# Splitting a weight once: a decoder block whose later token passes load the two parts of each weight from DRAM

## The chip, the cores and the metric

The kernel runs on one core of a Trainium2 chip. The metric is device time in microseconds (us) of one execution. Engines are named as the profile names them: PE (matmuls; PEld its weight loads), DVE (vector), ACT (scalar), POOL (GpSimd), SP (the queue that issues the DMAs).

## The reference

One conditioned decoder layer on 1024 tokens of width 1024, in float32. Cut to its matmuls and what stands between them:

```python
h = modulate(rmsnorm(x, norm1_g), sh1, sc1)
z = einsum('bsd,de->bse', h, w_in)         # pool channels | q | k | v | forget logits | gates A, B
y = sigmoid(gA) * causal_pool_mixer(u, w_pool, pool_scale) + sigmoid(gB) * forgetting_attention(q, k, v, log_f)
x = x + gt1 * einsum('bsd,de->bse', y, w_out)
h2 = modulate(rmsnorm(x, norm2_g), sh2, sc2)
q = einsum('bsd,dk->bsk', h2, w_query)     # 8 heads x 2 halves x 128
# scores against 128 sub-keys per half, top 16 of each half, top 16 of their sums: 16 of 16384 experts per head
x = x + gt2 * sum_k gelu(h2 . expert_u[idx_k]) * gate_k * expert_v[idx_k]
out = rmsnorm(x, final_g)
```

The modulation rows sh1 to gt2 are `c @ w_mod + b_mod`.

## The kernel before, in words

Float32 accuracy is had on PE by splitting each operand into a high part (ACT rounds it, line 232) and a low part (the remainder, line 233, on DVE or POOL), and by three matmuls for each product: high by high, high by low, low by high (`mm3`, lines 256 to 258).

Tokens go through the layer in three passes, `PHASES = ((0, 512), (512, 256), (768, 256))`. Each pass uses every weight of the layer once: 45 chunks of w_in, 8 of w_out, 16 of w_query. A chunk is a tile of 128 x 8 x 128 floats, 512 KB. `load_w` loads it into `wr` (line 244, two buffers), splits it into `wh` on ACT and `wl` on POOL (two buffers each; five for the head of the first pass, where the splits into `wl` run on DVE), and `proj` or `to_T` multiplies it with the tokens of the pass. So every chunk is loaded and split three times in a run, once for each pass.

A pass has a head (normalised and modulated columns, forget logits), an attention part for 8 pairs of heads (q, k, v, two gate chunks and half a pooling chunk for each pair), the output projection (into which the head of the next pass is written), and the query projection with the top-k on DVE. In the second and third pass background work is mixed in by a credit count in program order (`tick`): the choice of experts (`choose`, DVE) and the gate blocks (`gates`: products on POOL, line 942, comparisons on DVE, line 944, small matmuls and copies).

After the passes comes the dense stage: for the tokens of tiles 1 to 5 all 16384 experts are computed as dense matmuls. It uses `load_w` for 256 more chunks (`ut`, `vt`), while the experts of the other three tiles are gathered row by row in the background.

The order of instructions on each engine is set by the framework's scheduler, which orders by a timeline of its own; DMAs from SP are issued in one order, and each waits there for what it needs (buffer free, data written, and the completion of the eighth DMA before it on SP).

The names that matter below: `wr`, `wh`, `wl` (loaded chunk and its two parts), `wm` (rows of w_mod, for the modulation), line 565 (`mx`, the maximum over two parts of a score row, ahead of the exponential in line 567), line 570 (`dn`, the sum of two denominators), line 829 (`cand`, one step of the choice of experts).

Of the kernel before, what the change touches and what calls it, by code (L numbers as in the profile page):

```python
# [7 lines left out]
F = mybir.dt.float32  # L8
R = mybir.dt.float32r
# [37 lines left out]
def block_kernel(ctx: ExitStack, tc: tile.TileContext, I, out, dbg=None):  # L47
# [4 lines left out]
    dram = ctx.enter_context(tc.tile_pool(name="dram", bufs=1, space=bass.MemoryType.DRAM))  # L52
# [2 lines left out]
    psx = tc.alloc_tile_pool(name="psx", bufs=1, space=PS, reuse_waits="tile")  # L55
    sel = ctx.enter_context(tc.tile_pool(name="sel", bufs=1))
    gp = ctx.enter_context(tc.tile_pool(name="gp", bufs=1))
    W = {"i": 0, "m": 0}

    bg = {"todo": [], "credit": 0.0, "rate": 1.0}  # L60

# [98 lines left out]
    sh1, sc1, gt1, sh2, sc2, gt2 = (modc[:, 8 * i:8 * i + 8] for i in range(6))  # L160
# [66 lines left out]
    def mv(dst, src):  # L227
        fix = lambda a: a.bitcast(F) if a.dtype == R else a
        return nc.sync.dma_start(fix(dst), fix(src))

    def split(hi, lo, src, eng_lo):
        nc.scalar.activation(hi, src, AF.Copy)  # L232
        eng_lo.tensor_tensor(lo, src, hi.bitcast(F), op=OP.subtract)  # L233
# [3 lines left out]
    def wl_eng():  # L237
        wcount[0] += 1
        on_dve, per = wcount[1]
        return nc.vector if wcount[0] % per < on_dve else nc.gpsimd  # L240

    def load_w(src, eng=None):
        wr = W["p"].tile([128, 8, 128], F, name="wr", tag="wr", bufs=2)
        nc.sync.dma_start(wr, src)
        W["i"] = (W["i"] + 1) % (W["n"] + W["m"])
        wp, n = (W["p"], W["n"]) if W["i"] < W["n"] else (W["x"], W["m"])
        wh = wp.tile([128, 8, 128], R, name="wh", tag="wh", bufs=n)
        wl = wp.tile([128, 8, 128], R, name="wl", tag="wl", bufs=n)
        split(wh, wl, wr, eng or wl_eng())
        return wh, wl  # L250

    def w_row(name):
        return W["p"].tile([128, 8, 128], F, name=name, tag="wr", bufs=2).rearrange("p a b -> p (a b)")

# [11 lines left out]
    def head(p):  # L266
# [19 lines left out]
        c.tile, c.p_tile = tile_, p_tile  # L286
        c.xs = W["xs"] if p else x_rows(c)
        return c
# [42 lines left out]
    def x_cols(p, c):  # L331
        t0, n = PHASES[p]
        tiles, xs = load_cols(p, lambda: W["xq"].tile([128, D], F, name="xq", tag="xq", bufs=2))
        pt = spread(c, rs8[:, t0 // 128:(t0 + n) // 128])
# [5 lines left out]

    def to_T(c, xs, rsb, sc, sh, th, tl, srcs):

        ws = [load_w(src) for src in srcs]
        zs = [(z_tile() if i < 2 else s_tile("z"))[:, :c.n] for i in range(len(srcs))]

        def mm(k):
            for z, (wh, wl) in zip(zs, ws):
                mm3(z, wh[:, k], wl[:, k], th[:, k], tl[:, k], k == 0, k == 7)

        for k in range(8):  # L350
            full = c.tile("full", 3)
            if len(xs) < 8:
                src = pt_tile()[:, :c.n]
                for i in range(c.NQ):
                    nc.tensor.transpose(src[:, i * 128:(i + 1) * 128], xs[i][:, k * 128:(k + 1) * 128], ident)
            elif rsb is None:
                src = xs[k]
            else:
                src = full
                nc.vector.tensor_tensor(full, xs[k], rsb, op=OP.mult)  # L360
            nc.scalar.activation(full, src, AF.Identity, scale=sc[:, k:k + 1], bias=sh[:, k:k + 1])
            split(th[:, k], tl[:, k], full, nc.vector)
            if k > 1:
                mm(k - 2)
        mm(6)
        mm(7)
        return zs

    def head2(c):
        n, t0 = c.n, c.t0  # L370
        c.hTh = c.big.tile([128, 8, n], R, name="hTh", tag="A")
        c.hTl = c.big.tile([128, 8, n], R, name="hTl", tag="B")
        cols = (C_F,) + ((C_U, C_GA, C_GB, C_Q) if c.p == 0 else ())
        zs = to_T(c, c.xs, None, sc1, sh1, c.hTh, c.hTl, [I["w_in"][i] for i in cols])
        z = zs[0]
        c.pre = dict(zip(cols[1:], zs[1:]))

        zf, e1 = (c.tile("full", 3)[:16] for _ in range(2))
        nc.scalar.activation(zf, z[:16], AF.Identity, bias=bfc)
        nc.scalar.activation(e1, zf, AF.Abs)  # L380
        nc.scalar.activation(e1, e1, AF.Exp, scale=-1.0)
        nc.scalar.activation(e1, e1, AF.Ln, bias=1.0)
        nc.vector.scalar_tensor_tensor(e1, zf, 0.0, e1, op0=OP.min, op1=OP.subtract)
        nc.vector.tensor_tensor_scan(zf, e1, e1, flast, op0=OP.add, op1=OP.bypass)
        nc.vector.tensor_copy(flast, zf[:, n - 1:n])
        nc.vector.tensor_scalar(e1, zf, -1.0, None, op0=OP.mult)
        fhl = c.big.tile([48, n], R, name="fhl", tag="fhl", bufs=1)
        fh, fl = fhl[0:16], fhl[32:48]
        split(fh, fl, e1, nc.vector)
        mv(Fd[:, 0, t0:t0 + n], fh)  # L390
        mv(Fd[:, 1, t0:t0 + n], fl)
        if dbg and "F" in dbg:
            nc.sync.dma_start(dbg["F"][:, t0:t0 + n], zf)

    def proj(c, src, xh, xl):
        wh, wl = load_w(src)
        z = z_tile()[:, :c.n]
        for k in range(8):
            mm3(z, wh[:, k], wl[:, k], xh[:, k], xl[:, k], k == 0, k == 7)
        tick(24 * c.n * 0.00043)  # L400
        return z

    def w_in(c, i):
        return c.pre.pop(i) if i in c.pre else proj(c, I["w_in"][i], c.hTh, c.hTl)

    def u_unit(c, j):
        g, n = j // 2, c.n
# [50 lines left out]
    def phase(c, nxt):  # L458
        p, t0, n, NQ, qb0, KL, big = c.p, c.t0, c.n, c.NQ, c.qb0, c.KL, c.big
# [231 lines left out]
        tiles, x1 = load_cols(p, lambda: p_tile("x1"))  # L691
        ss = o_tile()[:, :n]
        sa = c.tile("sc", 1)
        for e in range(8):
            if nc_ and e == WO:
                head2(nc_)
            z = proj(c, I["w_out"][e], c.yh, c.yl)
            nc.vector.scalar_tensor_tensor(x1[e], z, gt1[:, e:e + 1], x1[e], op0=OP.mult, op1=OP.add)
            if e == 0:
                nc.scalar.activation(sa, x1[e], AF.Square)  # L700
                continue
            sq = c.tile("full", 3)
            nc.scalar.activation(sq, x1[e], AF.Square)
            if e < 7:
                nc.vector.tensor_tensor(sa, sa, sq, op=OP.add)
            else:
                nc.tensor.matmul(ss, onef, sa, start=True, stop=False)
                nc.tensor.matmul(ss, onef, sq, start=False, stop=True)
# [5 lines left out]
        rsb = rstd_T(c, ss)  # L714
        h2h = big.tile([128, 8, n], R, name="h2h", tag="A")
        h2l = big.tile([128, 8, n], R, name="h2l", tag="B")
        z0, = to_T(c, x1, rsb, sc2, sh2, h2h, h2l, [I["w_query"][0]])
        dl = [i for i in range(NQ) if DT0 <= qb0 + i < DT1]
        gl = [i for i in range(NQ) if i not in dl]
        if dl:  # L720
# [29 lines left out]
        tx = [sel.tile([128, PH, 2, 16], U32, name="mxi", tag="mxi", bufs=4) for _ in range(NQ)]  # L750
        for ch in range(16):
            h, half = ch // 2, ch % 2
            z = proj(c, I["w_query"][ch], h2h, h2l) if ch else z0
            if p == 2 and ch % 2:
                for x in range(2):
                    tc.keep_in_program_order(mv(W["h2"][x][:, ch // 2], h2dT[x][:, ch // 2]))
            q2 = c.tile("full", 3)
            nc.scalar.activation(q2, z, AF.Copy)
            ky = big.tile([128, 128], F, name="ky", tag="ky", bufs=2)
            nc.sync.dma_start(ky, I["keys"][ch])  # L760
            ps = pt_tile()[:, :n]
            for i in range(NQ):
                nc.tensor.matmul(ps[:, i * 128:(i + 1) * 128], q2[:, i * 128:(i + 1) * 128], ky,
                                 start=True, stop=True)
            sc = big.tile([128, n], F, name="sc", tag="sc", bufs=1)
            nc.scalar.activation(sc, ps, AF.Copy)
            for i in range(NQ):
                s_ = sc[:, i * 128:(i + 1) * 128]
                m_, x_ = tv[i][:, h, half], tx[i][:, h, half]
                tmp = sel.tile([128, 128], F, name="tmp", tag="tmp", bufs=2)  # L770
                nc.vector.max(m_[:, 0:8], s_)
                nc.vector.max_index(x_[:, 0:8], m_[:, 0:8], s_)
                nc.vector.match_replace(tmp, m_[:, 0:8], s_, -3e38)
                nc.vector.max(m_[:, 8:16], tmp)
                nc.vector.max_index(x_[:, 8:16], m_[:, 8:16], tmp)
        big.release()
        return nc_, [choose(qb0 + i, tv[i], tx[i]) for i in range(NQ)]

# [276 lines left out]
    c = head(0)  # L1055
# [5 lines left out]
    W["m"] = 3  # L1061
    head2(c)
    W["m"] = 0
    W["x"].release()
    u_unit(c, 0)
    g_unit(c, 0)
# [10 lines left out]
    c, ch = phase(c, next_head(1))  # L1077
# [5 lines left out]
    c, ch = phase(c, next_head(2))  # L1083
# [3 lines left out]
    c, ch = phase(c, lambda: None)  # L1087
# [66 lines left out]
```

## Time and profile before

| | before |
|---|---|
| median of 3 runs | 3461.2 us (3460.72 to 3464.09) |
| profiled execution | 3456.16 us, span 3454.5 us |
| mean granted PE clock | 0.967 |
| busy, share of the span | PE 92%, weight loads 88%, DVE 75%, ACT 39%, POOL 60% |
| HBM read, written | 778.90 MB, 77.23 MB |
| splits of weights on POOL (all stages) | 458, mean 2431 ns |
| splits of weights on ACT (all stages) | 463, mean 1059 ns |

The shares are means over the whole span. The three passes take the first 1590 us or so, the dense stage the rest; PE is busy all the time in the dense stage and less in the passes. The clock column of a view is the share of the full PE clock that was granted.

### The profile page before, as it was taken

The page shows a single profiled execution, that of the slowest core. Times are in us where ns is not written, and L with a number is a line of the kernel's source. Part 1 is how long each engine was busy: PE and PEld are TensorE (multiplying, and loading weights), DVE is VectorE, ACT ScalarE, POOL GpSimd, SP SyncE. Part 2 cuts the span into 40 slices and gives each one's busy share as a digit, 9 for nine tenths or more (in the row PEclk, how much of TensorE's full clock was granted, in tenths as well). Part 3 has the DMA queues.
Part 4 walks back from the last instruction along what each step waited for, and adds up shares of the span by engine and source line. Part 5 has one row for each costly group of instructions (what it writes and reads, how often), then busy time and mean ns, then how long its engine had stood idle before and what let it go on. Part 6 is the DMA issues. An engine that isn't in the chain of part 4 may idle for free. (4 is left out here: it accounts for less than half of the span.)

```text
span 3454.5 us, 57302 instructions
## 1 busy us (share of the span) xinstructions
PE 3179.9 (92%) x21232; PEld 3036.0 (88%) x21232; DVE 2582.4 (75%) x5472; ACT 1361.5 (39%) x2455; POOL 2089.0 (60%) x1466
## 2 busy tenths in 40 slices
PE   6999988778788789889999999999999999999995
PEld 4788777778778778879999999999999999999995
DVE  7855467998868997787876776776677767777677
ACT  5555543456565556663222222332232223222221
POOL 1233243346568445574677777777777777877774
PEclk9999999899899999989999999999999999999997
DMA  8633453345555545565698998899998998999897
GB/s 293 230 112 109 169 171 100 129 127 173 172 181 176 154 130 166 183 217 178 246 334 321 326 333 325 324 329 344 335 333 318 332 339 327 343 327 336 318 342 253
DMA packets 339095, 859.91 MB, mean 249 GB/s; under 512 B 30352, under 2 KB 146688, under 8 KB 336640
## 3 DMA queue, kind: packets, MB, share of 16 engines
q1 hardware_dynamic: 228224, 453.54, 39.5%
q0 software_dynamic: 110592, 402.70, 31.9%
q8 instruction: 168, 2.75, 0.3%
q14 instruction: 111, 0.91, 0.1%
HBM read 778.90 MB, written 77.23 MB: 248 GB/s over the span
## 5 line engine op out<-in xcount | busy, mean ns | idle before, releaser
L233 POOL TENSOR_TENSOR wl<-wr,wh 128x1024 fp32r<-128x1024 f32 x458 | 1113.1, 2431 | 851.7 <-ACT wh L232 751.4
L232 ACT ACTIVATE wh<-wr 128x1024 fp32r<-128x1024 f32 x463 | 490.0, 1059 | 1018.3 <-PE oT L257 528.8
L256 PE MATMUL oT<-ah,wh 128*128 128x320 f32 x2048 | 633.5, 310 | 5.7 <-ACT ah L232 5.7
L256 PE MATMUL z<-h2x,wh 128*128 128x320 f32 x2048 | 634.0, 310 | 1.3 <-DVE al L233 1.3
L257 PE MATMUL oT<-al,wh 128*128 128x320 f32 x2048 | 634.1, 310 | 0.2 <-DVE al L233 0.2
L258 PE MATMUL z<-h2x,wl 128*128 128x320 f32 x2048 | 634.1, 310 | 0.0
L257 PE MATMUL z<-h2x,wh 128*128 128x320 f32 x2048 | 633.9, 310 | 0.0
L258 PE MATMUL oT<-ah,wl 128*128 128x320 f32 x2048 | 633.9, 310 | 0.0
L896 DVE SCALAR_TENSOR_TENSOR acc<-g,dots,acc 128x1024 f32<-128x1024 f32 x381 | 489.6, 1285 | 113.4 <-DMA g<-peer_v,idx 110.7
L886 DVE SCALAR_TENSOR_TENSOR g<-g,h 128x1024 f32<-128x1024 f32 x384 | 461.3, 1215 | 89.4 <-DMA g<-peer_u,idx 88.3
L871 POOL DMA_INDIRECT g<-peer_u,idx x384 | 362.1, 943 | 130.0 <-issue 56.1
L871 POOL DMA_INDIRECT g<-peer_v,idx x384 | 362.0, 943 | 126.8 <-issue 46.4
L256 PE MATMUL z<-hTh,wh 128*128 128x256 f32 (+1 forms) x1080 | 365.3, 342 | 39.3 <-DVE ks L505 9.8
L256 PEld LDWEIGHTS oT<-ah,wh 128*128 128x128 f32 x2048 | 385.3, 188 | 6.2 <-ACT ah L232 6.2
L257 PEld LDWEIGHTS oT<-al,wh 128*128 128x128 f32 x2048 | 385.4, 188 | 0.9 <-DVE al L233 0.9
L256 PEld LDWEIGHTS z<-h2x,wh 128*128 128x128 f32 x2048 | 384.7, 188 | 1.5 <-DVE al L233 1.5
L258 PEld LDWEIGHTS oT<-ah,wl 128*128 128x128 f32 x2048 | 385.4, 188 | 0.0
L258 PEld LDWEIGHTS z<-h2x,wl 128*128 128x128 f32 x2048 | 384.7, 188 | 0.2 <-POOL wl L233 0.2
L257 PEld LDWEIGHTS z<-h2x,wh 128*128 128x128 f32 x2048 | 384.7, 188 | 0.0
L257 PE MATMUL z<-hTl,wh 128*128 128x256 f32 (+1 forms) x1080 | 360.7, 334 | 1.9 <-DVE hTl L233 1.9
L258 PE MATMUL z<-hTh,wl 128*128 128x256 f32 (+1 forms) x1080 | 360.8, 334 | 1.7 <-POOL wl L233 1.7
L942 POOL TENSOR_TENSOR o<-hi,lo 128x512 f32<-128x512 f32 x160 | 204.4, 1282 | 128.2 <-PE G L954 95.5
(268 smaller groups left out, 6035.0 us busy)
## 6 DMA issues: line engine op xcount, KB each, us to landing
wr<-w_in SPq DMA_DIRECT2D x135, 512.0 KB
wr<-ut SPq DMA_DIRECT2D x128, 512.0 KB
wr<-vt SPq DMA_DIRECT2D x128, 512.0 KB
Gd<-Gb SPq DMA_DIRECT2D x40, 1024.0 KB
Gg<-Gd SPq DMA_DIRECT2D x16, 2560.0 KB
wm<-w_mod SPq DMA_DIRECT2D x48, 512.0 KB
wr<-w_query SPq DMA_DIRECT2D x48, 512.0 KB
wr<-w_out SPq DMA_DIRECT2D x24, 512.0 KB
```

The source lines that it names most:

```text
L232: nc.scalar.activation(hi, src, AF.Copy)
L233: eng_lo.tensor_tensor(lo, src, hi.bitcast(F), op=OP.subtract)
L256: nc.tensor.matmul(ps, ah, bh, start=start, stop=False)
L257: nc.tensor.matmul(ps, ah, bl, start=False, stop=False)
L258: nc.tensor.matmul(ps, al, bh, start=False, stop=stop)
L871: d = nc.gpsimd.indirect_dma_start(out=g, out_offset=None, in_=table, in_offset=bass.IndirectOffsetOnAxis(ap=col, axis=0))
L886: nc.vector.scalar_tensor_tensor(g, g, 1.0, h2, op0=OP.mult, op1=OP.mult, accum_out=dots[:, k:k + 1])
L896: nc.vector.scalar_tensor_tensor(acc, g, dots[:, k:k + 1], acc, op0=OP.mult, op1=OP.add)
L942: nc.gpsimd.tensor_tensor(o2, hi[:, X, :, None].to_broadcast([128, 4, 8, 16]), lo[:, X, None, :].to_broadcast([128, 4, 8, 16]), op=OP.mult)
```

## The change

In the first pass a chunk is loaded and split as before, and both parts are then stored to DRAM tiles of their own. The store of a chunk is written in the program after the load and split of the next one (`store_parts(1)`); the last ones are flushed after the head and at the end of the pass. In the second and third pass the two parts are loaded straight into the matmul operands, two DMAs of 512 KB for each chunk, and nothing is split. The buffers used for these are those of `wh` and `wl` (two pairs) and, as a third pair, the two buffers of `wr`. The dense stage still uses `load_w` and its buffers.

```diff
+    kept, owed = {}, []
+
+    def store_parts(n=0):
+        while len(owed) > n:
+            for d, t in owed.pop(0):
+                mv(d, t)
+
+    def load_s(c, name, i):
+
+        if c.p == 0:
+            wh, wl = load_w(I[name][i])
+            kept[name, i] = [dram.tile([128, 8, 128], F, name=f"{name}{x}_{i}") for x in "hl"]
+            owed.append(list(zip(kept[name, i], (wh, wl))))
+            store_parts(1)
+            return wh, wl
+
+        W["s"] = (W["s"] + 1) % 3
+        tags = ("wr", "wr") if W["s"] == 2 else ("wh", "wl")
+        w = [W["p"].tile([128, 8, 128], R, name=tag, tag=tag, bufs=2) for tag in tags]
+        for t, d in zip(w, kept[name, i]):
+            mv(t, d)
+        return w
...
-        ws = [load_w(src) for src in srcs]
+        ws = [load_s(c, *src) for src in srcs]
...
-        wh, wl = load_w(src)
+        wh, wl = load_s(c, *src)
...
-            z = proj(c, I["w_out"][e], c.yh, c.yl)
+            z = proj(c, ("w_out", e), c.yh, c.yl)
...
+        store_parts()
         big.release()
...
     head2(c)
     W["m"] = 0
+    store_parts()
     W["x"].release()
```

Three places in the order of the instructions. First SP in the head of the first pass (`w_mod` are the rows for the modulation, `w_in` the weights). Before:

```order
L167 DMA wm_225<-w_mod 128x1024
L244 DMA wr_290<-w_in 128x1024
L244 DMA wr_296<-w_in 128x1024
L167 DMA wm_230<-w_mod 128x1024
L167 DMA wm_233<-w_mod 128x1024
L167 DMA wm_238<-w_mod 128x1024
```

and now (`w_inh_28` and `w_inl_28` are the kept parts of chunk 28):

```order
L167 DMA wm_225<-w_mod 128x1024
L229 DMA w_inh_28_284<-wh_280 128x1024
L229 DMA w_inl_28_285<-wl_281 128x1024
L244 DMA wr_296<-w_in 128x1024
L229 DMA w_inh_0_292<-wh_288 128x1024
L229 DMA w_inl_0_293<-wl_289 128x1024
L244 DMA wr_306<-w_in 128x1024
L167 DMA wm_230<-w_mod 128x1024
```

Four stores stand ahead of the next rows of w_mod, on the queue that issues both.

Second POOL in the attention part of the second pass, where the gate blocks begin (`hi`, `o2` are theirs, `wpl` is the pooling weight). Before:

```order
L233 TENSOR_TENSOR wl_7722<-wr_7719,wh_7721 128x1024
L942 TENSOR_TENSOR o2_6946<-hi_6940,lo_6941 128x512
...
L942 TENSOR_TENSOR o2_7011<-hi_6940,lo_6941 128x512
L233 TENSOR_TENSOR wpl_7795<-wpr_7792,wph_7794 128x256
L233 TENSOR_TENSOR wl_7842<-wr_7839,wh_7841 128x1024
L931 TENSOR_TENSOR hi_7227<-hi_7227,pairT_6928 128x128
L942 TENSOR_TENSOR o2_7079<-hi_7073,lo_7074 128x512
L233 TENSOR_TENSOR wl_7895<-wr_7892,wh_7894 128x1024
```

and now:

```order
L233 TENSOR_TENSOR wpl_6905<-wpr_6902,wph_6904 128x256
L955 TENSOR_TENSOR hi_7178<-hi_7178,pairT_7166 128x128
...
L966 TENSOR_TENSOR o2_7184<-hi_7178,lo_7179 128x512
...
L966 TENSOR_TENSOR o2_7237<-hi_7178,lo_7179 128x512
L233 TENSOR_TENSOR wpl_8017<-wpr_8014,wph_8016 128x256
L966 TENSOR_TENSOR o2_7247<-hi_7178,lo_7179 128x512
```

Rows that repeat the product are left out. The splits of 128 x 1024 are gone; the products of the gate blocks and the small split of the pooling weight stay.

Third SP at the end of the third pass, with what each DMA waits for (`DMAHW` is an earlier DMA; `Pool` and `PE` are the engines that must be done with the buffer; `h2x` are the columns for the dense stage, `ky` the sub-keys, `ut` the first dense weights). Before:

```order
L244 DMA wr_17171<-w_query 128x1024 [waits DMAHW0_49,Pool_49]
L760 DMA ky_17098<-keys 128x128 [waits DMAHW7_49,DMAHW6_49,PE_49]
L244 DMA wr_17223<-w_query 128x1024 [waits DMAHW1_49,Pool_49]
...
L229 DMA h2x0_15657<-h2dT0_150 128x640
...
L244 DMA wr_17289<-ut 128x1024 [waits DMAHW5_49,Pool_49]
```

and now:

```order
L229 DMA wr_17175<-w_queryh_14_5650 128x1024 [waits DMAHW6_49,PE_49]
...
L229 DMA wr_17176<-w_queryl_14_5651 128x1024 [waits DMAHW0_49]
L229 DMA wh_17225<-w_queryh_15_5720 128x1024 [waits DMAHW1_49,PE_49]
L229 DMA wl_17226<-w_queryl_15_5721 128x1024 [waits DMAHW2_49,PE_49]
L229 DMA h2x0_15705<-h2dT0_150 128x640 [waits DMAHW3_49]
...
L244 DMA wr_17289<-ut 128x1024 [waits PE_49]
```

Two loads stand where one stood, and they wait for PE instead of POOL; so does the first load of the dense stage, into a `wr` buffer that now holds a part of w_query's chunk 14.

More of the change, by code (lines that the diff above doesn't have):

```diff
@@ L57, in block_kernel @@
     gp = ctx.enter_context(tc.tile_pool(name="gp", bufs=1))
-    W = {"i": 0, "m": 0}
+    W = {"i": 0, "m": 0, "s": 0}
     bg = {"todo": [], "credit": 0.0, "rate": 1.0}
@@ L373, in head2 @@
         cols = (C_F,) + ((C_U, C_GA, C_GB, C_Q) if c.p == 0 else ())
-        zs = to_T(c, c.xs, None, sc1, sh1, c.hTh, c.hTl, [I["w_in"][i] for i in cols])
+        zs = to_T(c, c.xs, None, sc1, sh1, c.hTh, c.hTl, [("w_in", i) for i in cols])
         z = zs[0]
@@ L403, in w_in @@
     def w_in(c, i):
-        return c.pre.pop(i) if i in c.pre else proj(c, I["w_in"][i], c.hTh, c.hTl)
+        return c.pre.pop(i) if i in c.pre else proj(c, ("w_in", i), c.hTh, c.hTl)
     def u_unit(c, j):
@@ L716, in phase @@
         h2l = big.tile([128, 8, n], R, name="h2l", tag="B")
-        z0, = to_T(c, x1, rsb, sc2, sh2, h2h, h2l, [I["w_query"][0]])
+        z0, = to_T(c, x1, rsb, sc2, sh2, h2h, h2l, [("w_query", 0)])
         dl = [i for i in range(NQ) if DT0 <= qb0 + i < DT1]
@@ L752, in phase @@
             h, half = ch // 2, ch % 2
-            z = proj(c, I["w_query"][ch], h2h, h2l) if ch else z0
+            z = proj(c, ("w_query", ch), h2h, h2l) if ch else z0
             if p == 2 and ch % 2:
```

## The prediction

> **What bounds the kernel now.** I read the stretches of the run first, since the page's shares average stages with different limits. The columns are the stretch, its length, then busy time with counts of PE, weight loads, DVE, ACT and POOL, the granted clock, the DMA share and GB/s. I cut where the weights of w_out and w_query are first loaded: first pass 0 to 570 us, second 570 to 1085, third 1085 to 1590, dense stage after that.
>
> ```profile
> core 0: us, PE busy (x) PEld busy (x) DVE busy (x) ACT busy (x) POOL busy (x), PEclk, DMA share, GB/s
> 0.00:375.00 375.00, 338.94 (x1729) 276.76 (x1730) 234.77 (x450) 197.05 (x399) 104.90 (x57) 0.99 0.53 179
> 375.00:460.00 85.00, 77.25 (x392) 63.00 (x391) 42.66 (x56) 38.03 (x72) 26.78 (x12) 0.98 0.54 190
> 460.00:570.00 110.00, 101.01 (x505) 83.84 (x504) 79.45 (x409) 49.90 (x73) 42.09 (x19) 0.95 0.42 137
> 570.00:905.00 335.00, 264.23 (x1880) 249.89 (x1879) 307.77 (x942) 171.99 (x365) 159.52 (x100) 0.90 0.45 138
> 905.00:1005.00 100.00, 83.93 (x619) 79.12 (x617) 73.46 (x112) 61.36 (x100) 67.20 (x44) 0.93 0.59 178
> 1005.00:1085.00 80.00, 69.12 (x544) 66.23 (x545) 64.25 (x241) 46.31 (x78) 56.82 (x34) 0.98 0.61 190
> 1085.00:1423.00 338.00, 286.15 (x2135) 268.34 (x2135) 286.75 (x668) 200.11 (x388) 181.59 (x122) 0.92 0.53 159
> 1423.00:1494.00 71.00, 64.03 (x503) 60.08 (x502) 58.18 (x79) 43.14 (x72) 43.65 (x30) 0.98 0.57 175
> 1494.00:1590.00 96.00, 80.10 (x593) 76.17 (x594) 67.75 (x250) 54.33 (x93) 63.20 (x32) 0.91 0.73 238
> 1590.00:3454.00 1864.00, 1815.13 (x12346) 1812.58 (x12344) 1367.35 (x2269) 499.32 (x821) 1343.23 (x1024) 0.99 0.88 318
> ```
>
> The dense stage is bound by PE (97%) and the change leaves its instructions alone; it will start earlier or later as a block. The first pass is bound by PE too, at 90 to 92%. The two attention stretches of the later passes are different: from 570 to 905 DVE is busy 92% and PE 79%; from 1085 to 1423 both stand at 85%. So there the vector engine and the chains through it set the time.
>
> Next the instructions themselves, in order of time, at a place in the second pass (start, us, engine, line):
>
> ```profile
> 868.04 2.38 POOL L233 TENSOR_TENSOR wl<-wr,wh 128x1024 fp32r<-128x1024 f32 x1 [3.62 <-ACT wh L232]
> 868.10 2.34 DVE L570 TENSOR_TENSOR dn<-dn 128x1 f32<-128x1 f32 x1
> ```
>
> An addition of one element per partition takes 2.34 us, and ends 0.02 us after the split of a weight on POOL that had started 0.06 us before it. The two engines do not run these together: one holds the other off. How often that happens is in the minimum, median and maximum of a line, beside its mean in the groups (both from 570 to 1590 us; in the groups count, busy us, mean ns):
>
> ```profile
> L565 DVE TENSOR_TENSOR mx<-mx x64: 107/159/2383, 602.4 to 1445.8; 128x1 f32<-128x1 f32 x64
> L570 DVE TENSOR_TENSOR dn<-dn x64: 127/160/2343, 604.1 to 1448.6; 128x1 f32<-128x1 f32 x64
> L829 DVE SCALAR_TENSOR_TENSOR cand<-pk x192: 368/406/2636, 611.8 to 1270.7; 128x128 f32<-128x128 f32 x192
> L944 DVE TENSOR_TENSOR o<-iota,pairT x160: 664/692/2905, 725.7 to 1534.7; 128x512 f32<-128x512 f32 x160
> ...
> L944 DVE TENSOR_TENSOR o<-iota,pairT 128x512 f32<-128x512 f32 x160 | 167.8, 1052 | 34.1 <-PE G L954 33.9
> L829 DVE SCALAR_TENSOR_TENSOR cand<-pk 128x128 f32<-128x128 f32 x192 | 90.4, 608 | 0.1
> L565 DVE TENSOR_TENSOR mx<-mx 128x1 f32<-128x1 f32 x64 | 39.5, 617 | 0.5
> L570 DVE TENSOR_TENSOR dn<-dn 128x1 f32<-128x1 f32 x64 | 23.5, 368 | 21.6 <-ACT P L567 21.6
> ```
>
> Busy time less count times median is 57.1 + 12.5 + 29.3 + 13.3 = 112 us for these four lines alone, held off by weight splits or by the gating products (line 942). Done for every vector instruction of 570 to 1590 us (excess over its form's tenth percentile, put to the POOL instruction that overlaps it most), it gives 155 us held off by weight splits: 55 in 570:905, 13 in 905:1005, 13 in 1005:1085, 53 in 1085:1423, 14 in 1423:1494, 7 in 1494:1590; some 65 us more fall to other POOL work, which stays. Line 565 feeds the exponential, and PE waits for that. PE's longest waits there (total us, times, longest), and what the weights cost ACT and POOL:
>
> ```profile
> PE s L558 <- ACT P L567: 23.7, 14, 7.5
> PE s L558 <- DVE qs L493: 21.1, 5, 8.8
> PE G L954 <- ACT Gb L955: 18.5, 22, 3.7
> PE o L257 <- DVE tl L233: 18.3, 11, 4.8
> ...
> PE z L258 <- POOL wl L233: 6.9, 11, 1.2
> ...
> PE z L256 <- ACT wh L232: 5.8, 9, 1.6
> ...
> 570.00:1590.00 1020.00, 0.00 (x0) 142.70 (x135) 331.74 (x136) 0.92 0.54 165
> ```
>
> PE hardly waits for the split weights (6.9 + 5.8 us); it waits for vector results. The last row (busy DVE, ACT, POOL on the loaded weight) is the work that goes.
>
> **The change, part by part.** *Splits removed:* second and third pass use 69 weights each (45 of w_in, 8 of w_out, 16 of w_query), so 138 pairs of ACT and POOL splits go, 143 us of ACT and 332 us of POOL. Neither engine is a bound there (ACT 172 of 335, POOL 160 of 335), so the gain is what DVE and PE get: between 13 us (the direct waits) and 155 us (all held-off time on the path). How far a stretch shrinks I take from PE: in the first pass, where DVE has room, PE reaches 0.91 of a stretch (0.904, 0.909, 0.918). At 0.91, with the PE work as it is, 570:905 becomes 264.2/0.91 = 290 (45 less; DVE's own 308 − 55 = 253 fits at 87%), 905:1005 becomes 92 (8 less), 1005:1085 76 (4), 1085:1423 314 (24), 1423:1494 70 (1). The last stretch could lose 8, which I put at nothing because of its loads, below. Sum 82. Each gain is under the held-off time of its stretch.
>
> *Clock:* PE work itself shrinks where the granted clock was 0.90 and 0.92. If all of it came back, that is 10% of 264 and 8% of 286, 49 us; gaps from the remaining vector waits stay, so I take a fifth, 10 us (ends 0 and 49). The Trainium skill (TensorE: Matmul & The Clock Gate, "What's actually happening") says the clock halves after about 3.4 us of idling and returns after 3.4 us of work. By that rule alone, with most waits in the rows above averaging 1 to 4 us, shorter gaps would return most of the 49 and the sum would be some 30 us better; the trace gives the low clock only as means of stretches, so I stay with a fifth.
>
> *Stores added:* 138 stores of 524 KB, 72 MB, in the first pass. The rate that the queues reach:
>
> ```profile
> q1 hardware_dynamic: 228224, 453.54, 39.5%
> ...
> 10.00:20.00 10.00, 2.17 (x7) 1.00 (x8) 7.38 (x21) 6.21 (x16) 0.00 (x0) 1.00 0.98 366
> 20.00:60.00 40.00, 36.12 (x147) 26.55 (x147) 29.30 (x56) 21.32 (x33) 1.51 (x2) 1.00 0.87 298
> 60.00:150.00 90.00, 77.05 (x362) 60.64 (x363) 83.61 (x147) 45.63 (x90) 30.52 (x18) 0.94 0.75 262
> 150.00:375.00 225.00, 223.60 (x1217) 188.58 (x1216) 112.81 (x193) 120.22 (x254) 71.85 (x32) 1.00 0.35 113
> L244 SPq DMA_DIRECT2D wr<-w_in x17: 327/328/536, 8.9 to 148.3; - x17
> ```
>
> 453.54 MB in 39.5% of 3454.5 us is 332 GB/s for a queue kept full; 366 GB/s at a share of 0.98 is 373. The whole pass moves 179 × 375 + 190 × 85 + 137 × 110 = 98 MB now, 171 MB then: 457 to 514 us of transfers in 570, so it holds on average. Up to 150 us it does not: about 42 MB move there now, and the stores of 15 of the 17 weights loaded by then add 16 MB; 58 MB are 154 to 173 us, 4 to 23 too many. In the order the stores stand between the w_mod loads that the first normalised columns wait for, so I put the overflow on the path: 13. Behind 150 us (share 0.35, PE 99%) a weight's two stores take 1.05 MB / 332 GB/s = 3.2 us, beside its own matmuls. In 460:570 a weight has 101/16 = 6.3 us of PE; before its two buffers are overwritten the stores must have landed: I take 4 us for 375:570 (ends 0 and 25, 1 us for each of 24 weights).
>
> *Loads doubled:* 138 × 0.52 = 72 MB more in the later passes, and a load now waits for PE to be done with the weight three back, on the in-order SP queue, where a load waited for POOL before. Behind it stand keys and values of the next heads and gate blocks. 165 GB/s in 570:1590 become about 236, against 332: room on average. In 1494:1590, 238 × 96 = 22.8 MB and 14 × 0.52 = 7.3 MB are 30 MB, 91 us at 332 GB/s: that stretch cannot shrink by its 8 us. Elsewhere I take 9 us of late loads (ends 0 and 69, half a microsecond for each weight). The first weight of the dense stage now waits for PE to finish with w_query's chunk 14: 4 us once (ends 0 and 7).
>
> *Sum:* −82 − 10 + 13 + 4 + 9 + 4 = −62 us. The profiled execution took 3456.2 us (span 3454.5), 5.0 below the median 3461.2 of the three runs, so the median becomes 3399 us. From the bounds: −155 − 49 = −204 at best, −13 + 23 + 25 + 69 + 7 = +111 at worst; both ends need every term at its end.
>
> **The rivals.** *Held-off time is not on the path:* the vector instructions that are held off are mostly background (line 829) and what remains of POOL's products, which now run more densely, takes over. Then only the 13 us of direct waits and none of the clock return, against 30 us of costs: 17 us slower, 3478. Against it: DVE at 92% has nowhere to put 55 us.
> *Stores hold the buffers* (slower): in the first pass the split of a weight waits until the stores of the weight two back have landed. With PE at 90 to 99% there every microsecond of delay shows. With the 92 us of gain and the other 26 us of costs it decides from 66/64 = 1.0 us per weight for the 64 weights behind the head; at 2 us it costs 128 and the run takes 3461 − 92 + 26 + 128 = 3523. For it speaks SP, in order, waiting there for splits; against it 3.2 us of transfer under 6.3 us of PE. The Trainium skill (DMA: Bandwidth & Descriptors, "Anatomy of one DMA — SWDGE (gpsimd) path") puts about 2 us of fixed time on a transfer, most of it the confirmation of the write, heaviest in HBM. That would make 5.2 us of a pair of stores, still below 6.3, and the term would stay near its 4 us; no row here times a store.
> *Loads arrive late:* half a microsecond for each of 138 weights, 69 instead of 9, leaves a gain of 2 us: 3459, no change.
> *Larger gain:* all clock and half of the held-off time beyond my 82 come back: −62 − 39 − 37 = −138, 3323.
>
> **How the numbers follow.** Forecast (gain of 30 to 100 us) 0.62; larger gain 0.08; a gain of 7 to 30 us, part of the loads late, 0.12; no change 0.05; slower 0.13, of which held-off time 0.06 and stores 0.07. A measurement tells about 0.2%, 7 us, from no change: faster 0.82, same 0.05, slower 0.13. The range 3335 to 3450 leaves out the slower cases, no change and the far end of the larger gain.
>
> **What would show it.** In the profile after: no weight split on POOL in the second and third pass; means of lines 565 and 570 (shifted by 23 lines) near 0.2 to 0.3 us; DVE busy time of the two passes down by 130 us or more, and both passes together 70 to 95 us shorter. The first pass 10 to 25 us longer, most of it before 150 us, with a DMA share near 0.95 there. The dense stage's length within 5 us. I am wrong if lines 565 and 570 keep long maxima as often as now, if PE waits for DMA of wh, wl or wr by more than 20 us in the later passes, or if the first pass grows by over 60 us.

## The result, and the profile after

The changed kernel takes 3370.6 us (median of 4 runs, 3369.7 to 3374.2) against 3461.0 before: ratio 0.974 (95% interval 0.9726 to 0.9753), 90 us less. The forecast was 3399 us, 62 less. The profiled execution has a span of 3368.4 us, 86.1 less than before.

I cut both profiles where PE begins a stage: first pass up to its last matmul of the query projection, second and third pass up to theirs, dense stage to the end. Before (length, then busy PE, weight loads, DVE, ACT, POOL, clock, DMA share, GB/s):

```profile
0.00:580.80 580.80, 528.01 (x2674) 432.60 (x2675) 366.44 (x979) 287.26 (x547) 177.96 (x88) 0.98 0.50 171
580.80:1092.00 511.20, 413.48 (x3048) 393.24 (x3047) 442.38 (x1264) 282.48 (x542) 286.26 (x179) 0.92 0.51 156
1092.00:1591.30 499.30, 424.59 (x3182) 398.88 (x3181) 407.51 (x971) 292.47 (x545) 282.85 (x177) 0.93 0.58 176
1591.30:3454.50 1863.20, 1813.83 (x12335) 1811.28 (x12333) 1366.05 (x2260) 499.32 (x821) 1341.93 (x1024) 0.99 0.88 318
```

and after:

```profile
0.00:600.00 600.00, 538.64 (x2681) 441.89 (x2682) 355.53 (x979) 283.37 (x541) 170.32 (x89) 0.97 0.82 291
600.00:1055.90 455.90, 396.44 (x3045) 378.58 (x3044) 368.63 (x1265) 223.46 (x475) 117.70 (x104) 0.95 0.78 254
1055.90:1499.30 443.40, 402.53 (x3165) 382.56 (x3164) 329.07 (x944) 233.91 (x477) 125.67 (x111) 0.97 0.83 272
1499.30:3368.40 1869.10, 1816.21 (x12347) 1811.62 (x12345) 1370.36 (x2285) 500.03 (x824) 1343.17 (x1024) 0.99 0.88 318
```

First pass 19.2 us longer, second 55.3 and third 55.9 shorter, dense stage 5.9 longer: −86.1. In the two later passes together (1010.5 us before, 899.3 after) DVE is busy 152 us less, POOL 326 and ACT 118; PE, with all but 20 of the same 6230 matmuls, 39 less, at a clock of 0.95 and 0.97 instead of 0.92 and 0.93. DMA runs at about 0.8 in all three passes.

The lines that showed the vector engine held off, in the groups after (count, busy us, mean ns) and with minimum, median and maximum; 588 and 593 are what 565 and 570 were, 968 what 944 was:

```profile
L968 DVE TENSOR_TENSOR o<-iota,pairT 128x512 f32<-128x512 f32 x160 | 137.8, 866 | 31.3 <-PE G L978 31.0
L588 DVE TENSOR_TENSOR mx<-mx 128x1 f32<-128x1 f32 x64 | 15.4, 241 | 0.6
L593 DVE TENSOR_TENSOR dn<-dn 128x1 f32<-128x1 f32 x64 | 14.9, 233 | 25.5 <-ACT P L590 25.4
...
L588 DVE TENSOR_TENSOR mx<-mx x64: 115/155/1043, 618.8 to 1362.1; 128x1 f32<-128x1 f32 x64
L593 DVE TENSOR_TENSOR dn<-dn x64: 130/159/1021, 620.5 to 1363.8; 128x1 f32<-128x1 f32 x64
```

In these two one-element lines the maxima of 2.3 us are gone; what is left, 1.0 us, is about the length of one of POOL's gate products. Counted as in the prediction, no vector time is held off by weight splits in the later passes any more (about 155 us before), and some 66 us by the gate products (some 61 before). ACT's wait for `mx` ahead of the exponential and PE's longest waits, after (total us, times, longest):

```profile
ACT P L590 <- DVE mx L588: 38.1, 31, 3.4
```

```profile
PE G L978 <- ACT Gb L979: 13.6, 13, 3.7
PE s L581 <- ACT P L590: 10.4, 12, 3.3
...
PE s L581 <- DVE qs L516: 6.9, 1, 6.9
PE o L280 <- DVE tl L233: 6.3, 8, 1.8
PE z L279 <- DMA wh<-w_inh: 4.5, 2, 3.1
...
PE z L281 <- DMA wl<-w_inl: 3.8, 4, 2.0
PE z L279 <- DMA wh<-w_queryh: 3.5, 3, 2.0
PE z L281 <- DMA wl<-w_queryl: 2.9, 4, 0.8
...
PE z L281 <- DMA wr<-w_queryl: 1.5, 2, 1.1
```

The waits for the exponential and for vector results are a third to a half of what they were (exponential 23.7, `qs` 21.1, `tl` 18.3 us). Waits for late loads have appeared, 16 us in the rows shown.

### The profile page after: what moved, and what is told of

The parts are those of the page before. It is cut to its first block, busy times and chain, and to the rows that moved or that the text cites. A ratio compares the mean times of both kernels' runs of the same rounds, so it can differ in the third digit from the quotient of the medians.

```text
span 3368.4 us, 57444 instructions
## 1 busy us (share of the span) xinstructions
PE 3153.8 (94%) x21232; PEld 3014.7 (89%) x21232; DVE 2423.6 (72%) x5472; ACT 1240.8 (37%) x2317; POOL 1756.9 (52%) x1328
## 5 line engine op out<-in xcount | busy, mean ns | idle before, releaser
L233 POOL TENSOR_TENSOR wl<-wr,wh 128x1024 fp32r<-128x1024 f32 x320 | 776.5, 2427 | 624.8 <-ACT wh L232 553.1
L232 ACT ACTIVATE wh<-wr 128x1024 fp32r<-128x1024 f32 x325 | 344.2, 1059 | 900.4 <-PE oT L280 520.7
L279 PE MATMUL z<-hTh,wh 128*128 128x256 f32 (+1 forms) x840 | 288.9, 348 | 24.5 <-ACT hTh L232 8.3
L281 PE MATMUL z<-hTh,wl 128*128 128x256 f32 (+1 forms) x840 | 287.1, 342 | 3.8 <-DMA wl<-w_inl 3.8
L280 PE MATMUL z<-hTl,wh 128*128 128x256 f32 (+1 forms) x840 | 286.7, 341 | 1.4 <-DVE hTl L233 1.3
```

Of the source, the lines that this page charges most:

```text
L279: nc.tensor.matmul(ps, ah, bh, start=start, stop=False)
L280: nc.tensor.matmul(ps, ah, bl, start=False, stop=False)
L281: nc.tensor.matmul(ps, al, bh, start=False, stop=stop)
```

## The experiments

My theory: the later passes gain because DVE is no longer held off by POOL's splits. The rivals: relief of ACT, a shorter way of the weights to PE, or another order; and for the first pass, transfers against buffers held. "Passes" below are second plus third, cut as above: 1010.5 us before, 899.3 in the changed kernel.

How far the order alone moves a pass is seen in two kernels whose later passes have the very instructions of the kernel before (stores alone, and the w_mod background spread in the kernel before; both below): 1021.5 and 1024.8 us. Differences of up to about 14 us in the passes are therefore ascribed to nothing here. The first pass of the ten kernels that keep all stores takes 589.4 to 600.0 us (580.8 before). The kernel before, timed again beside each group of runs, took 3459.5 to 3461.7 us.

**Stores alone.** First pass as in the change, later passes load and split.

```diff
+        return load_w(I[name][i])
         W["s"] = (W["s"] + 1) % 3
```

> First pass as in the changed kernel (both parts stored, 72 MB), later passes as before (load and split again). Theory (the stores cost by transfers that do not fit into the first 150 us, and nothing later): the first pass is 19 us longer than before, as in the changed kernel (600 against 581 us), the later passes as before, 3480 us (3472 to 3488). Rival (part of the 19 us comes from the second pass's double loads inside the first pass's tail, or stores still under way disturb the second pass): 3465 to 3472, or above 3490.

Measured 3478.6 us, ratio 1.0062 (1.0040 to 1.0085), 17 us more than before. The total is as expected; the place is only partly so: the first pass takes 590.5 us (9.7 more), the later passes 1021.5 (11 more, within what the order does).

**Loads alone.** Five chunks are stored, and the later passes load these five over and over, so they work with other weights.

```diff
-            owed.append(list(zip(kept[name, i], (wh, wl))))
+            if name == "w_in" and i in (C_K + 3, C_V + 3, C_Q + 4, C_K + 4, C_V + 4):
+                kept[len(kept)] = ...
...
-        for t, d in zip(w, kept[name, i]):
+        for t, d in zip(w, kept[W["r"]]):
```

> Only five chunks are stored, in the middle of the first pass, and all 138 uses of the later passes load those five in turn, so the later passes work with other weights; same instructions, same bytes loaded. Theory (gain of the later passes and cost of the stores simply add): 3371 less 19, 3352 us (3344 to 3360), first pass within 4 us of before, second and third pass 111 us shorter than before together as in the changed kernel. Rival (the later passes gain because the first pass leaves them a better start, or the stores did not cost what the first pass lost): 3362 to 3375.

Measured 3356.5 us, ratio 0.9702 (0.9686 to 0.9719), 105 less than before. First pass 584.1, later passes 899.1, the changed kernel's to 0.2 us. So gain and cost add: −105 + 17 = −88 against −90. Without the other stores the kernel is 14 us faster.

**POOL's work put back.** In the changed kernel, for each loaded chunk:

```diff
             mv(t, d)
+        scr = gp.tile([128, D], F, name="scr", tag="g", bufs=GBUFS).rearrange("p (a b) -> p a b", b=128)
+        nc.gpsimd.tensor_tensor(scr, w[0].bitcast(F), w[1].bitcast(F), op=OP.subtract)
```

> The changed kernel, with one POOL subtraction of 128x1024 put back for each loaded chunk of the later passes; it reads the two loaded parts and writes a tile that nobody reads, so nothing waits for its result. Theory (vector instructions are held off while POOL runs such an instruction, and that set the time): 130 to 155 us of DVE time are held off again, lines for mx and dn have means of 0.4 us or more, and 80 to 115 us of the gain go: 3451 to 3486 us. Rival (the gain came from ACT being relieved, from the weights no longer passing through ACT and POOL before PE, or from the later passes' other order): 3371 to 3386 us.

Measured 3484.5 us, ratio 1.0073 (1.0049 to 1.0097): 114 us over the changed kernel, all of the gain and more. Passes 1021.1 us. Its groups, its minimum, median and maximum, and ACT's wait for `mx`:

```profile
L970 DVE TENSOR_TENSOR o<-iota,pairT 128x512 f32<-128x512 f32 x160 | 166.0, 1042 | 16.1 <-PE G L980 15.6
L590 DVE TENSOR_TENSOR mx<-mx 128x1 f32<-128x1 f32 x64 | 34.5, 539 | 0.6
L595 DVE TENSOR_TENSOR dn<-dn 128x1 f32<-128x1 f32 x64 | 26.8, 419 | 25.7 <-ACT P L592 25.4
...
L590 DVE TENSOR_TENSOR mx<-mx x64: 128/160/2310, 616.8 to 1467.9; 128x1 f32<-128x1 f32 x64
```

```profile
ACT P L592 <- DVE mx L590: 94.3, 40, 8.6
```

The maxima of 2.3 us are back, some 154 us of vector time are held off by this instruction, and ACT waits 94 us for `mx` (100.1 before, 38.1 in the changed kernel). Nothing reads what the instruction writes. POOL's own gate products queue behind it too, but PE waits only 3.6 us for them here (7.3 in the changed kernel). The theory holds; that the instruction also waits for the loads is taken up below.

**Half of it, and a copy instead.** The same with `scr[:, :4]` (128x512), and with `nc.gpsimd.tensor_copy(scr, w[0].bitcast(F))`.

> As the kernel that puts POOL's subtraction back, but on half of each chunk (128x512). Theory (time held off goes with the length of POOL's instruction): between 40 and 70 us of the 114 return, 3411 to 3441. Rival (it is the number of encounters, not their length): 90 us or more, 3461 or more.

> As the kernel that puts POOL's work back, but with a copy of one loaded part (one input) in place of the subtraction of two. If a POOL instruction holds vector instructions off for its own length whatever it is, its length in the profile gives the loss: with 1.0 to 1.3 us each, as for the half subtraction, 3411 to 3441. If only a POOL instruction with two inputs does, 3371 to 3385.

Measured 3407.6 us (ratio 0.9849, 0.9831 to 0.9868) and 3405.4 (0.9846, 0.9825 to 0.9867), 37 and 35 over the changed kernel; both fall a few us short of the expected 3411, since their first passes are 8 and 10 us shorter than the changed kernel's. The lengths of POOL's instruction:

```profile
L274 POOL TENSOR_TENSOR scr<-wh,wl 128x512 f32<-128x512 f32 x89 | 121.1, 1361 | 224.6 <-DMA wl<-w_inl 171.8 <-DMA wl<-w_queryl 41.3 <-DMA wl<-w_outl 8.6
```

```profile
L274 POOL COPY scr<-wh 128x1024 f32<-128x1024 f32 x88 | 100.8, 1146 | 241.6 <-DMA wh<-w_inh 175.2 <-DMA wh<-w_queryh 49.3 <-DMA wh<-w_outh 14.4
```

| POOL per chunk | mean length | vector time held off by it | passes | over the changed kernel |
|---|---|---|---|---|
| none | | 0 | 899.3 us | |
| copy, one input | 1.12 us | 31 us | 938.1 | 39 |
| subtraction of a half | 1.36 us | 55 us | 946.6 | 47 |
| subtraction of the whole | 2.48 us | 154 us | 1021.1 | 122 |

The loss grows with the time held off, at 0.8 to 0.9 us for each us in the two subtractions and 1.3 in the copy, where what the order may do is a third of the loss. A copy with one input holds DVE off as well.

**ACT's work put back.** `nc.scalar.activation(scr, w[0].bitcast(F), AF.Copy)` for each chunk.

> The changed kernel, with one ACT copy of 128x1024 put back for each loaded chunk of the later passes, into a tile that nobody reads (138 times 1.06 us, 146 us of ACT). Theory (ACT's time was not what the later passes gained from): at most 12 us longer, 3371 to 3383 us. Rival (ACT's relief made the exponentials and the high parts of the probabilities earlier, and this is half of the gain or more): 3415 us or more.

Measured 3404.8 us, ratio 0.9848 (0.9827 to 0.9870), 34 over the changed kernel; passes 939.0 (40 more). That is between my two cases: ACT was worth more than I gave it. Read the other way, this is the change without its gain on ACT: with POOL's splits gone and ACT's work kept (though PE no longer waits for its result), the passes are 71.5 us shorter than before, and taking ACT's work away as well gives another 39.7.

**The waits without the work.** One element per partition on POOL and on ACT for each chunk, and the same on ACT alone:

```diff
+        nc.gpsimd.tensor_tensor(scr[:, 0, :1], w[0][:, 0, :1].bitcast(F), w[1][:, 0, :1].bitcast(F), op=OP.subtract)
+        nc.scalar.activation(scr[:, 1, :1], w[0][:, 0, :1].bitcast(F), AF.Copy)
```

> The changed kernel with, for each loaded chunk of the later passes, a POOL subtraction and an ACT copy of one element per partition of the loaded tiles: the waits and the hold on the buffers of the two kernels that put the work back, without its length. Theory (the length of the work did it): within 8 us of the changed kernel, 3363 to 3379. Rival (the instructions that were put back delayed the loads, because a buffer stays taken until POOL or ACT, in order, gets to it): a third or more of the 114 us of the POOL work, 3409 or more.

> The changed kernel with only the ACT copy of one element per partition of each loaded chunk. The kernel with this and POOL's one element took 24 us more than the changed one without adding any length. Theory (ACT issues in order, so an instruction that waits there for a load keeps the exponentials and copies behind it): most of the 24 us are ACT's, 3386 to 3398 us. Rival (POOL issues in order too, and its gate products wait behind the load): 3366 to 3378 us.

Measured 3395.1 us (ratio 0.9805, 0.9786 to 0.9825) and 3394.9 (0.9812, 0.9792 to 0.9831): 24 to 25 us over the changed kernel, passes 927.5 us in both (28 more). So POOL's waits add nothing to ACT's, and most of what ACT's work costs (28 of 40 us in the passes) comes without its length; the other 12 are within what the order does. ACT in the second of them:

```profile
L274 ACT ACTIVATE scr<-wh 128x1 f32<-128x1 f32 x89 | 18.0, 202 | 106.4 <-DMA wh<-w_inh 80.7 <-DMA wh<-w_queryh 19.6 <-DMA wh<-w_outh 6.1
L274 ACT ACTIVATE scr<-wr 128x1 f32<-128x1 f32 x44 | 8.8, 201 | 46.5 <-DMA wr<-w_inh 32.0 <-DMA wr<-w_queryh 10.7 <-DMA wr<-w_outh 3.7
```

ACT stands idle 153 us ahead of these instructions, waiting for loads, with what follows queued behind; the instructions themselves take 27. The expectation of the first (within 8 us) failed, that of the second held. Whether the wait itself or the order that the scheduler makes around it carries the 28 us was not separated; it is twice what the order did elsewhere. POOL's one element alone was not run, so what POOL's waits cost where ACT has none is not shown. But the half subtraction waits for the same loads as the whole one and costs 47 us in all, so 75 of the whole one's 122 us at least go with its length.

**The split on DVE, without any DRAM copy.** In the kernel before, `WL = ((0, 1), (1, 1), (1, 1))`.

> The kernel before, with the low parts of the later passes split on DVE instead of POOL and nothing stored or kept. DVE takes on 138 times 1.22 us (its time for this split in the head), 168 us, and is no longer held off for 155 us by splits. Theory (DVE's time, own or held off, sets these passes): within 25 us of before, 3436 to 3486. Rival (what counts is that POOL's split is slow and late for PE): 3400 to 3430, since the split takes half as long.

Measured 3435.7 us, ratio 0.9935 (0.9913 to 0.9956), 24 less than before; passes 979.9 (31 less). DVE's busy time in the passes is 854 us (850 before): its own work has taken the place of the time held off, as expected, at the edge of the range. It is worth a quarter of the change. This also speaks against POOL's slow and late work as the cause, since POOL is relieved of these splits here too.

**Two attempts on the first pass.** The w_mod background spread (cost 5 instead of 2 in `mod_rest`), in the changed kernel and in the kernel before; and the head's ten stores written behind the head (`if not W["m"]: store_parts(1)`).

> The changed kernel with the background loads and products of w_mod spread over the attention part of the first pass (cost 5 in place of 2 for each of 32). Theory (the first pass loses by transfers that do not fit before 150 us, where these loads run too): the DMA share between 60 and 150 us falls below 0.85, and the first pass gets 5 to 15 us shorter: 3356 to 3366. Rival (the loss is in the head before 60 us, or in buffers held by stores): 3367 to 3375.

> The same spreading in the kernel before, whose DMA share between 60 and 150 us is 0.75 but whose DVE is busy 93% there. If the spreading helps by relieving DVE rather than the DMA queues, it gains here as much as in the changed kernel; if it is the queues, this stays within 4 us of before.

> The changed kernel with the stores of the five head chunks written in the program behind the head instead of within it. Theory (these ten stores stand before the last w_mod rows of the head and delay them): the attention of the first pass starts about 8 us earlier and the run takes 3361 to 3368. Rival (they then delay the first attention loads or the tiles that take over their buffers by as much): 3368 to 3378.

Measured 3371.8 us (ratio 0.9743, 0.9727 to 0.9759), 3475.6 (1.0041, 1.0027 to 1.0056) and 3369.3 (0.9733, 0.9718 to 0.9749). Neither version beats the changed kernel by more than the intervals. The first passes are 10.6 and 7.4 us shorter, the later passes 8 us longer in both; spread, the loads did not lower the DMA share between 60 and 150 us (0.90 against 0.89, where I expected less than 0.85), so this could not tell transfers from the rest. In the kernel before, spreading makes the run 14 us slower, where I had named a gain or no change; all of it is in the later passes (1024.8 us), which the edit does not touch.

## Why the prediction was right, and where it was off

**Right in the mechanism and the sign.** Vector instructions held off by POOL's splits set the two attention parts: putting back POOL's work alone, read by nobody, takes back more than the gain. The rival that the time held off is not on the path fell with it. Of the signs named, no split is left on POOL in the later passes, the two means are 0.24 and 0.23 us, and DVE's busy time fell by 152 us. Three came out otherwise: the two passes shrank by 111 us and not by 70 to 95, most of the first pass's loss does not stand before 150 us, and the dense stage grew by 5.9 us, where I had said within 5.

**First pass: +17 forecast, +19.2 measured** (+8.6 to +19.2 over the ten kernels with these stores). The transfers do pile up early, as computed, but most of that does not last. The changed kernel, by stretches (the kernel before is in the prediction):

```profile
20.00:60.00 40.00, 30.75 (x120) 22.77 (x121) 26.91 (x51) 13.84 (x19) 0.74 (x1) 1.00 0.96 370
60.00:150.00 90.00, 79.93 (x374) 64.17 (x373) 61.73 (x108) 52.14 (x103) 25.36 (x15) 0.91 0.89 308
150.00:420.00 270.00, 258.64 (x1381) 216.26 (x1380) 147.06 (x268) 138.15 (x290) 81.69 (x35) 0.98 0.80 281
```

Between 20 and 60 us the queues are full (0.96, 370 GB/s) and PE gets 30.8 us of work instead of 36.1. From 60 to 150 us it makes up for part of this (374 matmuls instead of 362): from 20 to 150 us it does 494 matmuls where the kernel before does 509. The 15 missing are an estimated 3 us, at the 0.18 us of a matmul between 150 and 375 us of the kernel before (223.6 us for 1217). So of the 13 us put on the path before 150 us about 3 are left, and about 16 are lost later, where the sum had 4. That the total came out near the sum is luck, also of the order of the instructions: the same stores cost 9 to 16 us in the other nine kernels.

The rival that stores hold the buffers did not come in its size: 16 us over the 64 weights behind the head would be 0.25 us each, where 1.0 decides, and after 150 us PE stays at 96% (99% before), at twice the DMA share. What the 16 us are stays open: moving the head's stores, or the w_mod loads, shortened the first pass by 7 and 11 us and gave it back later. No row shown here times a store, so the prediction's 5.2 us for a pair of them stay unmeasured.

**Later passes: −83 forecast (−82 − 10 + 9), −111 measured.** The sign and the path were right; three terms of the sum were mis-sized, the first two too small a gain and the third too small a cost.

The first is the step "Neither engine is a bound there, so the gain is what DVE and PE get", by which ACT's part was nothing beyond PE's direct waits (12.7 us with POOL's). ACT's work put back costs 34 us (40 in the passes), 24 of the 34 by waiting instructions alone. ACT's busy share (172 of 335 us) could not show this: what seems to count is what stands behind the waiting split in ACT's order, the exponentials and the copies that PE waits for. Without ACT's part the passes gain 71.5 us, against 83 forecast. ACT's 40 and POOL's 122 do not add up to the 111: each was put back alone, and they overlap. With POOL's work in place, ACT's is worth nothing (1021.1 us without it, 1010.5 to 1024.8 with it).

The second is the clock. I took a fifth of 49 us, 10. The 49 were counted in the two attention parts alone; cut from the start of a pass to its output projection, these are, before and after:

```profile
581.00:951.00 370.00, 289.96 (x2103) 275.43 (x2101) 336.46 (x951) 198.71 (x411) 182.43 (x118) 0.90 0.49 149
1092.00:1443.00 351.00, 297.39 (x2218) 278.18 (x2217) 295.00 (x659) 206.99 (x408) 184.34 (x122) 0.93 0.53 158
...
600.00:933.00 333.00, 282.09 (x2120) 267.50 (x2119) 288.90 (x954) 167.02 (x373) 81.74 (x73) 0.93 0.72 231
1056.00:1357.50 301.50, 279.90 (x2205) 264.56 (x2203) 237.05 (x658) 169.55 (x364) 82.79 (x78) 0.97 0.80 253
```

PE's busy time fell there by 25 us (587.4 to 562.0), half of the 49. In the whole passes it fell by 39 (838.1 to 799.0 us), where the clock column puts the time lost at 76 us before (0.08 of 511.2 and 0.07 of 499.3) and 36 after: half here too. So my fifth was too little; most of it, which the prediction would have by the rule of the Trainium skill quoted there, was too much. Against that, PE's share did not reach the 0.91 on which the 82 us rest: 799.0 of 899.3 us is 0.889.

The third is the late loads, 9 us forecast. PE's waits on loaded weights shown above are 16.2 us in 15 waits, near the 20 us that I had named as a sign of being wrong. The last stretch of the third pass, which I said could not shrink because of its transfers, did not shrink: its query projection takes 76.4 us (76.5 before). Whether its transfers are why is not shown: PE waits for weights there only some 5 us.

**Dense stage: +4 forecast, +5.9 measured.** Its first matmul follows the last of the third pass after 2.5 us (0.1 before), as the order suggested; the other 3.5 us I did not foresee (12 more matmuls fall into it).

## What to carry to other kernels

Look in the trace for the shortest instructions of an engine with a long maximum: an addition of one element that takes as long as the neighbour's instruction is held off by it, and its engine's busy share then counts waiting as work. Work on an engine with room to spare can still set the time, by holding off another engine or, as it seems here, by standing as a wait ahead of what others need; put it back alone, at full, half and no length, to see which. Loading a prepared operand twice as large can cost less than preparing it again, where the queues have room and the first pass can carry the stores.

## What the runs showed of the hardware that I had not expected

A POOL copy with one input holds vector instructions off too: 132 copies of 1.12 us held off 31 us, 132 subtractions of 1.36 us 55 us, 133 of 2.48 us 154 us. For each us of POOL's instruction that is 0.21, 0.31 and 0.47 us, so the time held off grows faster than the length. Whether the copy holds off less than a subtraction of the same length was not tried. The same instructions in the later passes took 1010.5, 1021.5 and 1024.8 us after edits to the first pass alone, so the scheduler's order seems to be worth over 1% of these passes, or 0.4% of the kernel, by itself.
